# One tile and one rhythm for the modulation sums of a hybrid mLSTM and delta-rule block

## The chip, the cores and the metric

The kernel runs on one core of a Trainium2 chip. The metric is device time in microseconds of one execution. The core has TensorE (PE, with its weight loads as PEld), VectorE (DVE), ScalarE (ACT), GpSimd (POOL) and SyncE (SP); each works through its own instructions in the order in which the built program lists them, and they wait for each other through semaphores. In this kernel SP issues the loads of weights, POOL and ACT issue the smaller transfers to and from scratch memory in HBM.

## The reference, cut to what matters

One layer of a bidirectional encoder with 256 tokens and a width of 2048. Everything is float32.

```python
mod = c_act @ ada_w + ada_b                       # 6 x 2048 sums over 2048
shift_m, scale_m, gate_m, shift_f, scale_f, gate_f = jnp.split(mod[:, None, :], 6, axis=-1)
h = rms_norm(x, norm_mix_w) * (1 + scale_m) + shift_m
proj = h @ w_in                                   # 20 608 columns
...                                               # mLSTM (4 heads) -> y_a, gated delta rule (16 heads) -> y_b
x = x + gate_m * ((g_a * y_a + g_b * y_b) @ w_out)
hf = rms_norm(x, norm_ffn_w) * (1 + scale_f) + shift_f
gt, up = jnp.split(hf @ w_gate_up, 2, axis=-1)
x = x + gate_f * ((jax.nn.silu(gt) * up) @ w_down)
return rms_norm(x, norm_final_w)
```

The vector `mod` has six parts of 2048. Parts 0 and 1 are needed for the first projection. Part 2 (`gate_m`) is first used where the branch outputs are merged, parts 3 and 4 at the entrance of the feed-forward network (FFN), part 5 (`gate_f`) after it. The delta rule needs the inverse of a unit lower triangular matrix for each chunk and head.

## The kernel before, in words

**Products.** Each product in float32 is made of three products in a faster format: an operand is split into a high part (ACT copies it, `wh`) and a low part (DVE subtracts, `wl`). A weight tile of 1 MB (`raw`, three buffers) is split in two halves of 128 x 1024; each half takes one ACT copy, one DVE subtraction and 12 or 24 matmuls. A *job* (`fjob` for 128 columns, `tjob` for 512) is a generator that yields after every half; `fill(n)` advances the waiting jobs by n halves. `wh` and `wl` have three buffers each, so the splits can run up to three halves ahead of PE.

**Modulation sums.** Parts 2 to 5 are not made on PE. A row block of the transposed weights (128 x 2048, 1 MB) is loaded on SP's queue (`ask`, L116) and multiplied by the activated `c` and summed along the row in one DVE instruction (`add`, L124). There are 64 of them, 16 for each part. `pump` is called by every job after each half. With one tile, a sum is made when one is owed, the load is older than two halves and `held` is not set; the load for the next sum is asked for in the half after. `every` is the number of halves after which a sum is owed, 0 for none.

**Stages.** After the first projection (in which PE waits for loads) the delta rule goes in four groups g of four heads. Each group has: phase 1 of its heads (in the *pairs* of the group before), the inversion of its 32 x 32 blocks, and two pairs of heads (`gdn_phase2`). The inversion (`gdn_invert`, L704 and L710) is a chain of 60 small DVE instructions on the tile `uu`. Its last rows are stored by POOL to `inv_d` (L696), loaded again by POOL as the square tile `cg` (L723), transposed on DVE (L725) and mixed into the tile `R` (L729, L730, two instructions for each of two halves of `R`). The pair's first product on PE, `p1` (L761), reads the first half of `R` and the second, `p2` (L770), the other half. While the inversion and this round trip last, PE works on jobs: `invert` fills during the inversion, and `fill(8)` behind it.

Then comes the *border*: two mLSTM heads, the split of the delta rule's output (`obl`), the product with `w_branch_b` (`yb`), two more mLSTM heads, the product with `w_branch_a` (`ya`), the product with `w_out` (`o`), the FFN (`gt`, `up`, `d`).

**Sums by stage, before.** `every` is 1 in the pairs, 0 in inversions and `fill(8)`, 0 again at the start of the border, 1 from the third mLSTM head on, 4 in `ya` with a pool `sr` of three tiles that are asked for ahead, by explicit calls of `sums()` in the `o` jobs, and 8 in the FFN with one tile.

**Order.** A tile framework puts the instructions of each engine in an order by its own estimate of times; what is wrapped in `order(...)` keeps its place relative to the program. The order that was built, not the source, is what the engines follow.

Of the kernel before, what the change touches and what calls it, by code (L numbers as in the profile page):

```python
# [9 lines left out]
F32 = mybir.dt.float32  # L10
# [5 lines left out]
P = 128  # L16
T = 256
D = 2048
# [34 lines left out]
def hybrid_block(ctx: ExitStack, tc: tile.TileContext, xr, nfr, crow, pk_d, cst_d, ada2, ada4, win0, winb, wint, wba, wbb, wo, wgu, wd, out, dbg=None):  # L53
# [3 lines left out]
    def pool(stack, name, bufs=1, **kw):  # L57
        return stack.enter_context(tc.tile_pool(name=name, bufs=bufs, **kw))
# [3 lines left out]
    rows_p = pool(ctx, "rows")  # L62
# [9 lines left out]
    def order(ins, yes=True):  # L72

        return tc.keep_in_program_order(ins) if yes else ins
# [30 lines left out]
        order(S.activation(row_c[:, g * 512 : (g + 1) * 512], pc_, AF.Silu))  # L105


    room = [(rows_p, "ada", 1, 1)]
    asked, unasked, age = [], [], [0]

    def ask():

        pl, tag, bufs, _ = room[0]
        part, b = unasked.pop(0)
        raw = pl.tile([P, D], F32, tag=tag, bufs=bufs, name=f"ada{part}_{b}")
        order(nc.sync.dma_start(raw, ada4[part - 2, b]))  # L116
        asked.append((part, b, raw))
        age[0] = 0

    def add():  # L120

        part, b, raw = asked.pop(0)
        c = part * KB + b
        order(V.scalar_tensor_tensor(raw, raw, 1.0, row_c[:, :D], ALU.mult, ALU.mult, accum_out=mod[:, c : c + 1]))  # L124
        if b == KB - 1:
            c = slice(part * KB, part * KB + KB)
            V.tensor_tensor(mod[:, c], mod[:, c], pk[:, PK_ADAB + c.start : PK_ADAB + c.stop], ALU.add)
# [11 lines left out]
    def settle(keep=0, only=None):  # L139

        now = [f for f in behind if only is None or f.__name__ == only]
        for f in now[: len(now) - keep]:
            behind.remove(f)
            f()

    count, every = [0], [0]
    owed, held = [0], [False]

    def sums(n=1):

        while n and (unasked or asked):
            while unasked and len(asked) < room[0][3]:
                ask()
            add()
            n -= 1

    def pump():
        count[0] += 1
        age[0] += 1
        if every[0] and count[0] % every[0] == 0:  # L160
            owed[0] = 1
        if room[0][3] > 1:
            if owed[0]:
                owed[0] = 0
                sums()
        elif asked:
            if owed[0] and age[0] > 2 and not held[0]:
                owed[0] = 0
                add()
        elif unasked and every[0]:  # L170
            ask()

    def fjob(name, src, done):
# [95 lines left out]
    def fill(n=1):  # L269

        while n and fills:
            if next(fills[0], None):
                n -= 1
            else:
                fills.pop(0)
# [90 lines left out]
    def z_job(g, early=0):  # L366
        def done(ps):
            szs[g] = evp.tile([P, 2, 512], F32, tag="sz", bufs=1, name=f"sz{g}")
            for t in range(2):
                S.activation(szs[g][:, t], ps[t], AF.Silu)  # L370
        return tjob(f"z{g}", [wint[g, u] for u in range(4)], hh, hl, done, early)
# [121 lines left out]
    with ExitStack() as s0:  # L493
# [18 lines left out]
        def loads(b):  # L512
            ra = [w0.tile([P, D + 2], F32, tag="ra", bufs=5, name=f"ra{b}_{i}") for i in range(2)]
            raw = st.tile([P, N0, P], F32, tag="raw", bufs=3, name=f"raw0_{b}")
            for i in range(2):
                order(nc.sync.dma_start(ra[i], ada2[b, :, i]))
            order(nc.sync.dma_start(raw, win0[b]))
            return ra, raw
# [10 lines left out]
        ra, raw = loads(0)  # L529
# [18 lines left out]
        for b in range(KB):  # L548
            if b:
                ra, raw = loads(b)  # L550
# [137 lines left out]
    def gdn_invert(g):  # L688

        uu = uus.pop(g)  # L690
        tmp = bk.tile([64, 256], F32, tag="utmp", bufs=1, name=f"utmp{g}")
        inv = inv_d[g].rearrange("j b (x h) i -> h (b x) j i", h=GRP)

        def store(rows):
            for e in range(GRP):
                G.dma_start(inv[e, :, rows], uu[16 * e : 16 * e + 16, rows])  # L696

        yield
        order(V.memset(uu.rearrange("p j i -> p (j i)")[:, ::33], 1.0))
        size = 0  # L700
        for i in range(30, 0, -1):
            w = 31 - i
            t3 = tmp[:, 0 : i * w].rearrange("p (j c) -> p j c", j=i)
            order(V.tensor_tensor(  # L704
                t3,
                uu[:, 0:i, i : i + 1].broadcast_to([64, i, w]),
                uu[:, i : i + 1, i + 1 :].broadcast_to([64, i, w]),
                ALU.mult,
            ))
            order(V.tensor_tensor(uu[:, 0:i, i + 1 :], uu[:, 0:i, i + 1 :], t3, ALU.add))  # L710
            if i == 16:
                store(slice(16, 32))
            size += i * w + 125
            if size > 720:
                size = 0
                yield
        store(slice(0, 16))
# [300 lines left out]
    def invert(g):  # L1018
        gen = gdn_invert(g)
        next(gen)  # L1020
        fill(4 if g else 6)
        for _ in gen:
            fill(1)

    invert(0)
    for g in range(4):
        blocks = gdn_blocks(g)
        next(blocks)
        fill(8)
        next(blocks)  # L1030
        fill(1)
        pairs = [gdn_phase2(g, p) for p in range(2)]
        if g == 3:
            settle()
            sf.close()
            mq["pool"] = pool(sq_, "mq", side="right")
            first2 = [mlstm(h) for h in range(2)]
            for c in first2:
                next(c)
        every[0] = 1  # L1040
        for p in range(2):
            pieces = stream(4 * g + 2 * p + 4)
            for n in range(1, 10):

                held[0] = n < 4
                if p == 0:
                    next(blocks, None)
                next(pairs[p], None)
                if g == 3 and n == (8, 4)[p]:
                    next(first2[p])  # L1050
                for _ in range(last[n] if g == 3 else second[n] if p else after[n]):
                    next(pieces)
            for _ in pairs[p]:
                pass

            if g < 3:
                while 4 * g + 2 * p + 5 not in heads:
                    next(pieces)
        if g < 3:
            fills.insert(0, z_job(g + 1))  # L1060
            every[0] = owed[0] = 0
            invert(g + 1)
    settle()
    sx.close()
# [53 lines left out]
            yield from y_b(g)  # L1118

    o4s = [o_load(g) for g in range(2)]  # L1120
    every[0] = owed[0] = 0
    cores = steps(*first2)
    fill(1)
    next(cores)
# [19 lines left out]
    o_split(3, o4s[3])  # L1144
    fill(2)
    drive(cores, 3)
    every[0] = 1
    drive(steps(mlstm(2), mlstm(3)), 3)
    fill(1000)
    mgh, mgl = big(bigC, F32R, "mgh"), big(bigC, F32R, "mgl")  # L1150
    sm_.close()
    sr_ = ExitStack()
    if asked:
        add()
    room[0] = (pool(sr_, "sr"), "sr", 3, 3)
    gm = room[0][0].tile([P, D], F32, name="gm")
    dgs = {}

    def row_diag(part, g, rp):
        ms = mods[:, part == 5]  # L1160
        if not g:
            m = mod[:, part * KB : (part + 1) * KB]
            V.tensor_copy(ms[:, 0], m)
            V.tensor_tensor(ms[:, 1], m, ms[:, 0].bitcast(F32), ALU.subtract)
        dg = dgs[part, g] = rp.tile([P, 2, 4, P], F32R, tag="dg", bufs=2, name=f"dg{part}_{g}")
        for i in range(2):
            V.tensor_tensor(
                dg[:, i], ident.unsqueeze(1).broadcast_to([P, 4, P]),
                ms[:, i, 4 * g : 4 * g + 4].bitcast(F32).unsqueeze(2).broadcast_to([P, 4, P]), ALU.mult,
            )  # L1170
# [6 lines left out]
            PE.matmul(pr, onesr, woven(dg[:, i]), start=i == 0, stop=i == 1)  # L1177
        S.activation(woven(dst[:, g * 512 : (g + 1) * 512]), pr.rearrange("p (c h) -> p c h", h=2), AF.Copy)

    every[0] = 4  # L1180
    for g in range(4):
        for i, _ in enumerate(y_a(g)):
            if g and i == 3:
                merged(g - 1, mgh, mgl)
            if i in (1, 5) and g < 2:
                row_diag(2, 2 * g + i // 4, room[0][0])
            if i in (3, 7) and g < 2:
                row_spread(2, 2 * g + i // 4, gm)
    every[0] = 0


    def o_job(g, front=None):
# [112 lines left out]
    for g in range(4):  # L1305
        if g == 3:
            root()
        for i, _ in enumerate(o_job(g, front_o if g == 3 else None) if g else o_first, 0 if g else 2):
            if i in ((4, 7), (2, 5), (2, 5), (0, 2))[g]:
                sums()  # L1310
            if g == 3 and i == 4:
                sums(P)
                V.scalar_tensor_tensor(
                    affn, mod[:, 4 * KB : 5 * KB], 1.0, pk[:, PK_NFFN : PK_NFFN + KB], ALU.add, ALU.mult
                )
    if dbg is not None and "x1" in dbg:
        G.dma_start(dbg["x1"], x1)
    room[0] = (rows_p, "ada", 1, 1)
    ada_parts(5)
    sw.close()  # L1320
    sr_.close()
# [73 lines left out]
    for j in range(FB // 4):  # L1395
# [4 lines left out]
        for e2 in range(2):  # L1400
            px = gps(f"pxf{j}_{e2}")
            for e in range(2):
                f = 2 * e2 + e
                for t in range(2):
                    PE.transpose(px[:, e * T + t * P : e * T + (t + 1) * P], sg[:, t, f * P : (f + 1) * P], ident)
            b = 4 * j + 2 * e2
# [156 lines left out]
```

## Time and profile before

| | us |
|---|---|
| median of 3 runs | 1973.03 |
| lowest and highest run | 1969.95, 1974.28 |
| the profiled execution's own time | 1974.3 |
| its span | 1972.4 |
| PE busy | 1929.4 |
| DVE busy | 1405.5 |
| ACT busy | 1030.0 |
| the 64 modulation sums on DVE | 146.0 |
| mean granted clock of TensorE | 0.994 |

The profile's page says what each engine did in the span, which chain of work ended last, and which groups of instructions were the costliest. A busy PE is not a PE at its peak: matmuls overlap, and a matmul of 128 x 512 lasts 0.38 us while the next starts 0.22 us later. Where the start-to-start time grows, PE has lost time, and the view of waits tells for whom. The view of windows gives the busy time of each engine in a stretch and the granted clock there (1.00 is full speed).

### The profile page before, as it was taken

What the parts mean: (1) busy time and instruction counts of PE and PEld (TensorE: products, weight loads), DVE (VectorE), ACT (ScalarE), POOL (GpSimd) and SP (SyncE); (2) the same over time, 40 slices, a digit from 0 to 9 for tenths busy, and PEclk for the clock granted to TensorE, in tenths of its full rate; (3) what the DMA queues carried; (4) which work ended last, traced back from release to release, by engine and by line L of the source; (5) the groups of instructions that cost most, each with busy time, mean ns of one, the idle gap of its engine ahead of it and who ended that gap; (6) DMA issues with size and microseconds to landing.
All of it is one profiled execution on the core that took longest, in us unless ns stands there. A gap on an engine that the chain in (4) does not pass through costs nothing.

```text
span 1972.4 us, 27079 instructions
## 1 busy us (share of the span) xinstructions
PE 1929.4 (98%) x10418; PEld 1703.5 (86%) x10418; DVE 1405.5 (71%) x2067; ACT 1030.0 (52%) x1555; POOL 116.5 (6%) x211
## 2 busy tenths in 40 slices
PE   8999999999999999999999999999999999999998
PEld 6878889998998899889787888888888888888886
DVE  6779887887888798866577878866665665555554
ACT  3137656764766577565544444644444444444444
POOL 0001210111001010110100000200000000000000
PEclk9999999999999999999999999999999999999999
DMA  9987676766566666586777888566676665565663
GB/s 399 420 349 226 184 249 240 252 214 208 203 217 213 237 218 229 192 296 246 277 282 266 323 317 330 191 252 238 238 265 241 237 238 205 197 213 197 208 199 142
DMA packets 78962, 485.64 MB, mean 246 GB/s; under 512 B 10585, under 2 KB 15969, under 8 KB 24433
## 3 DMA queue, kind: packets, MB, share of 16 engines
q1 hardware_dynamic: 63216, 450.69, 62.9%
q0 software_dynamic: 8160, 17.88, 4.5%
q10 hardware_dynamic: 7458, 15.36, 2.1%
q8 instruction: 81, 1.33, 0.3%
q14 instruction: 47, 0.39, 0.1%
HBM read 467.07 MB, written 16.82 MB: 245 GB/s over the span
## 4 chain that ended last, share of the span: by engine, by line
PE 81%; DVE 8%; DMA 6%; ACT 2%; issue 1%; POOL 0%; ACTq 0%; SPq 0%; DVEq 0%; POOLq 0%
PE acc_gt L234 4%; PE acc_gt L235 4%; PE acc_gt L236 4%; PE acc_up L236 4%; PE acc_up L235 4%; PE acc_up L234 4%; PE acc_d L236 4%; PE acc_d L235 4%; PE acc_d L234 4%; DMA ra<-ada 3%; PE acc_b L187 2%; PE acc_b L188 2%; PE acc_b L189 2%; PE acc_o L236 2%; PE acc_o L234 2%; PE acc_o L235 2%
## 5 line engine op out<-in xcount | busy, mean ns | idle before, releaser
L215 DVE TENSOR_TENSOR wl_d<-raw_d,wh_d 128x1024 fp32r<-128x1024 f32 x88 | 107.7, 1224 | 105.9 <-ACT wh_d L213 105.9
L215 DVE TENSOR_TENSOR wl_up<-raw_up,wh_up 128x1024 fp32r<-128x1024 f32 x88 | 107.7, 1224 | 100.2 <-ACT wh_up L213 100.1
L215 DVE TENSOR_TENSOR wl_gt<-raw_gt,wh_gt 128x1024 fp32r<-128x1024 f32 x88 | 108.1, 1229 | 80.2 <-ACT wh_gt L213 80.2
L187 PE MATMUL acc_b<-hh,wh_b 128*128 128x256 f32 x576 | 163.0, 283 | 0.6 <-ACT wh_b L182 0.6
L189 PE MATMUL acc_b<-hh,wl_b 128*128 128x256 f32 x576 | 159.6, 277 | 0.8 <-DVE wl_b L184 0.8
L188 PE MATMUL acc_b<-hl,wh_b 128*128 128x256 f32 x576 | 159.2, 276 | 0.0
L213 ACT ACTIVATE wh_d<-raw_d 128x1024 fp32r<-128x1024 f32 x88 | 92.9, 1056 | 126.5 <-PE acc_d L235 117.7
L213 ACT ACTIVATE wh_gt<-raw_gt 128x1024 fp32r<-128x1024 f32 x88 | 92.9, 1056 | 118.6 <-PE acc_gt L235 71.1
L213 ACT ACTIVATE wh_up<-raw_up 128x1024 fp32r<-128x1024 f32 x88 | 92.8, 1055 | 108.1 <-PE acc_up L235 77.1
L124 DVE SCALAR_TENSOR_TENSOR ada<-ada,crow 128x2048 f32<-128x2048 f32 x64 | 146.0, 2284 | 0.0
L234 PE MATMUL acc_gt<-wh_gt,hfh 128*128 128x512 f32 x352 | 135.6, 385 | 0.6 <-ACT hfh L1350 0.6
L235 PE MATMUL acc_gt<-wh_gt,hfl 128*128 128x512 f32 x352 | 134.9, 383 | 0.0
L236 PE MATMUL acc_gt<-wl_gt,hfh 128*128 128x512 f32 x352 | 134.1, 381 | 0.0
L234 PE MATMUL acc_up<-wh_up,hfh 128*128 128x512 f32 x352 | 133.4, 379 | 0.0
L235 PE MATMUL acc_up<-wh_up,hfl 128*128 128x512 f32 x352 | 133.4, 379 | 0.0
L236 PE MATMUL acc_up<-wl_up,hfh 128*128 128x512 f32 x352 | 133.4, 379 | 0.0
L234 PE MATMUL acc_d<-wh_d,ffh 128*128 128x512 f32 x344 | 130.5, 379 | 0.0
L235 PE MATMUL acc_d<-wh_d,ffl 128*128 128x512 f32 x344 | 130.5, 379 | 0.0
L236 PE MATMUL acc_d<-wl_d,ffh 128*128 128x512 f32 x344 | 130.4, 379 | 0.0
L561 PE MATMUL first<-x,raw 128*128 128x256 f32 x512 | 114.5, 382 | 7.2 <-ACT x L555 7.2
L561 PEld LDWEIGHTS first<-x,raw 128*128 128x128 f32 x512 | 96.0, 190 | 25.7 <-ACT x L555 13.3
L189 PEld LDWEIGHTS acc_b<-hh,wl_b 128*128 128x128 f32 x576 | 111.3, 193 | 1.0 <-DVE wl_b L184 1.0
(383 smaller groups left out, 5263.1 us busy)
## 6 DMA issues: line engine op xcount, KB each, us to landing
ada<-ada SPq DMA_DIRECT2D x64, 1024.0 KB, 6.0
raw_gt<-wgu SPq DMA_DIRECT2D x44, 1024.0 KB, 4.9
raw_up<-wgu SPq DMA_DIRECT2D x44, 1024.0 KB, 4.9
raw_d<-wd SPq DMA_DIRECT2D x44, 1024.0 KB, 4.9
raw_b<-winb SPq DMA_DIRECT2D x36, 1024.0 KB, 5.3
ra<-ada SPq DMA_DIRECT2D x32, 1025.0 KB, 15.8
raw<-win SPq DMA_DIRECT2D x16, 1024.0 KB, 14.5
raw_z<-wint SPq DMA_DIRECT2D x16, 1024.0 KB, 5.0
```

Of the source, the lines that this page charges most:

```text
L124: order(V.scalar_tensor_tensor(raw, raw, 1.0, row_c[:, :D], ALU.mult, ALU.mult, accum_out=mod[:, c : c + 1]))
L187: PE.matmul(o, wh[:, k], woven(hh[:, kk]), start=kk == 0, stop=False)
L188: PE.matmul(o, wh[:, k], woven(hl[:, kk]), start=False, stop=False)
L189: PE.matmul(o, wl[:, k], woven(hh[:, kk]), start=False, stop=kk == KB - 1)
L213: order(S.activation(wh, raws[u][:, k0 : k0 + 2], AF.Copy), early)
L215: order(V.tensor_tensor(wl, raws[u][:, k0 : k0 + 2], wh.bitcast(F32), ALU.subtract), early)
L234: order(PE.matmul(ps[t], xh[:, kk, c], woven(wh[:, k]), start=kk == 0, stop=False), early and steps > 1)
L235: PE.matmul(ps[t], xl[:, kk, c], woven(wh[:, k]), start=False, stop=False)
L236: PE.matmul(ps[t], xh[:, kk, c], woven(wl[:, k]), start=False, stop=kk == last)
L561: PE.matmul(first[o], raw[:, o], x[:, b], start=b == 0 and o % 2 == 0, stop=b == KB - 1 and o % 2 == 1)
```

## The change

The pool of three tiles is gone, and so are `room` and the explicit `sums()` in the `o` jobs. One tile serves all sums, and `pump` alone makes them. The rhythm is kept on from the moment a group's inversion has been emitted (`every` 1, `held` off before `fill(8)`), through the border, `yb`, `ya` and the first `o` job. A new number `calm` says how many halves must pass between a sum and the load for the next one: 3 in the pairs of groups 0 to 2, otherwise 1; so a sum is due every six halves there and every four halves elsewhere.

```diff
-    room = [(rows_p, "ada", 1, 1)]
@@ ask
-        pl, tag, bufs, _ = room[0]
         part, b = unasked.pop(0)
-        raw = pl.tile([P, D], F32, tag=tag, bufs=bufs, name=f"ada{part}_{b}")
+        raw = rows_p.tile([P, D], F32, tag="ada", name=f"ada{part}_{b}")
@@
-    owed, held = [0], [False]
+    owed, held, calm = [0], [False], [1]
@@ sums
-            while unasked and len(asked) < room[0][3]:
+            if not asked:
                 ask()
@@ pump
-        if room[0][3] > 1:
-            if owed[0]:
-                owed[0] = 0
-                sums()
-        elif asked:
+        if asked:
             if owed[0] and age[0] > 2 and not held[0]:
-                owed[0] = 0
+                owed[0] = age[0] = 0
                 add()
-        elif unasked and every[0]:
+        elif unasked and every[0] and age[0] >= calm[0]:
             ask()
@@ for g in range(4):
         blocks = gdn_blocks(g)
         next(blocks)
+        every[0], held[0] = 1, False
         fill(8)
@@
-        every[0] = 1
+        calm[0] = 3 if g < 3 else 1
         for p in range(2):
@@
             every[0] = owed[0] = 0
+            calm[0] = 1
             invert(g + 1)
@@ the border
     o4s = [o_load(g) for g in range(2)]
-    every[0] = owed[0] = 0
+    held[0] = False
@@
     drive(cores, 3)
-    every[0] = 1
     drive(steps(mlstm(2), mlstm(3)), 3)
@@ before ya
-    if asked:
-        add()
-    room[0] = (pool(sr_, "sr"), "sr", 3, 3)
-    gm = room[0][0].tile([P, D], F32, name="gm")
+    sr = pool(sr_, "sr")
+    gm = sr.tile([P, D], F32, name="gm")
@@ ya
-    every[0] = 4
     for g in range(4):
...
-    every[0] = 0
@@ o jobs
-            if i in ((4, 7), (2, 5), (2, 5), (0, 2))[g]:
-                sums()
-            if g == 3 and i == 4:
+            if g == 3 and i == 3:
+                every[0] = owed[0] = 0
                 sums(P)
```

More of the change, by code (lines that the diff above doesn't have):

```diff
@@ L1185, in hybrid_block @@
             if i in (1, 5) and g < 2:
-                row_diag(2, 2 * g + i // 4, room[0][0])
+                row_diag(2, 2 * g + i // 4, sr)
             if i in (3, 7) and g < 2:
                 row_spread(2, 2 * g + i // 4, gm)
-    every[0] = 0
     def o_job(g, front=None):
@@ L1317, in hybrid_block @@
         G.dma_start(dbg["x1"], x1)
-    room[0] = (rows_p, "ada", 1, 1)
     ada_parts(5)
```

## The prediction

> **What bounds the kernel now.** I read the page first, then PE's waits from 290 to 1260 us (the delta rule to the entrance of the FFN, where every moved sum lies), then DVE and PE in order of time at the border and behind the inversions.
>
> ```profile
> span 1972.4 us, 27079 instructions
> PE 1929.4 (98%) x10418; PEld 1703.5 (86%) x10418; DVE 1405.5 (71%) x2067; ACT 1030.0 (52%) x1555; POOL 116.5 (6%) x211
> PE 81%; DVE 8%; DMA 6%; ACT 2%; issue 1%; POOL 0%; ACTq 0%; SPq 0%; DVEq 0%; POOLq 0%
> L124 DVE SCALAR_TENSOR_TENSOR ada<-ada,crow 128x2048 f32<-128x2048 f32 x64 | 146.0, 2284 | 0.0
> ada<-ada SPq DMA_DIRECT2D x64, 1024.0 KB, 6.0
> ```
>
> PE carries 81% of the chain that ended last. The change neither adds nor removes a matmul, a sum or a load: it can only change what PE waits for. In the stretch these are PE's waits that the change touches (total, times, longest):
>
> ```profile
> PE acc_ya L236 <- DVE wl_ya L215: 3.8, 2, 2.2
> PE acc_z L234 <- ACT wh_z L213: 2.5, 1, 2.5
> PE acc_ma L236 <- DVE wl_ma L215: 1.6, 2, 0.9
> PE acc_o L236 <- DVE wl_o L215: 1.1, 2, 0.8
> PE p L770 <- DVE pt L762: 1.0, 1, 1.0
> PE acc_b L189 <- DVE wl_b L184: 0.8, 1, 0.8
> PE acc_b L187 <- ACT wh_b L182: 0.6, 1, 0.6
> PE pb L819 <- DVE r L820: 0.6, 2, 0.3
> ```
>
> All of it is 12.0 us, and two of the waits cost more than they show, because the granted clock falls behind them:
>
> ```profile
> 1083.74 0.59 PE L1177 MATMUL row<-dg,onesr 128*128 128x512 f32 x2
> 1086.49 0.93 PE L236 MATMUL acc_ya<-wl_ya,hah 128*128 128x512 f32 x2 [2.15 <-DVE wl_ya L215]
> 793.28:796.69 3.41, 3.24 (x7) 2.15 (x8) 1.86 (x2) 3.33 (x9) 1.97 (x4) 0.50 0.11 19
> 1086.85:1090.20 3.35, 3.35 (x9) 2.60 (x8) 3.15 (x4) 1.14 (x2) 0.00 (x0) 0.50 0.98 306
> ```
>
> In the last two rows (windows) the third number from the right is the clock: 0.50 for 3.4 us after the waits of 2.5 and 2.15 us. In 3.4 us at half clock only half the work gets done, so each such window costs 1.7 us more. [...]
>
> **The change, part by part.** Positions are those of the changed program as built.
>
> *The ya border, removed.* Three sums stand back to back ahead of a split:
>
> ```profile
> 1080.80 2.29 DVE L124 SCALAR_TENSOR_TENSOR ada<-ada,crow 128x2048 f32<-128x2048 f32 x1
> 1083.01 2.28 DVE L124 SCALAR_TENSOR_TENSOR ada<-ada,crow 128x2048 f32<-128x2048 f32 x1
> 1085.22 1.22 DVE L215 TENSOR_TENSOR wl_ya<-raw_ya,wh_ya 128x1024 fp32r<-128x1024 f32 x1
> ```
>
> A sum costs DVE 2.21 us from start to start. In the changed order one sum stands between two splits, and the `dg` instructions that held up the second `wl_ya` stand behind later splits. Gain: the row of 3.8 and one half-clock window, -5.5. With one sum per four halves the splits keep their lead on PE; if they did not, the same 3.8 would return. The `o` jobs, with nine sums before, keep two; those that leave stood beside residual additions: -0.3, the smaller of the two waits in the `acc_o` row.
>
> *Pairs.* Groups 0 to 2 keep four of six sums; the one ahead of `r` (L820) goes: -0.6. Nothing else there is PE's wait on a sum.
>
> *Behind the inversions, added.* Group 0 gets two sums in DVE's idle time, and one split moves ahead of a mix of `R`: -0.7, the first of the `acc_ma` waits. In groups 1 and 2, though, the built order puts two sums *inside* the end of the inversion, and more splits too (group 1: two more, group 2: three more). DVE has no room there, and much behind it (DVE's busy time is the third one):
>
> ```profile
> 443.00:475.00 32.00, 30.24 (x139) 25.84 (x139) 30.59 (x66) 16.79 (x18) 2.25 (x4) 1.00 0.60 202
> 475.00:492.00 17.00, 17.00 (x117) 15.90 (x115) 8.03 (x10) 6.66 (x10) 4.21 (x8) 1.00 0.72 241
> ```
>
> Group 1, the end of the inversion, the square's arrival, the first half of `R`, the load's issue, `p1`:
>
> ```profile
> 469.62 1.21 DVE L215 TENSOR_TENSOR wl_o<-raw_o,wh_o 128x1024 fp32r<-128x1024 f32 x1
> 474.64 0.17 DVE L710 TENSOR_TENSOR uu<-uu,utmp 64x30 f32<-64x30 f32 x1
> 489.73 0.71 DVE L725 STREAM_TRANSPOSE cg<-cg 128x512 f32<-128x512 f32 x1 [3.62 <-DMA cg<-inv_d]
> 490.71 0.48 DVE L730 SCALAR_TENSOR_TENSOR R<-cg,cst,R 128x256 f32<-128x256 f32 x1
> 482.32 1.99 POOL L723 DMA_DIRECT2D cg<-inv_d  x4 [5.00 <-DMA inv_d<-uu]
> 471.23 0.38 PE L236 MATMUL acc_o<-wl_o,hh 128*128 128x512 f32 x1
> 491.79 0.98 PE L761 MATMUL p<-R,cc 128*128 128x32 f32 x8
> ```
>
> Before, `R` is ready at 491.2 and PE comes to `p1` at 491.8. After, the inversion ends 2 x 2.21 + 2 x 1.13 = 6.7 us later (1.13 is a split's pitch on a full DVE: two take 2.35 in a row below, one 1.22), and with the same 15.1 us to the square `R` is ready at 497.9. The split of 469.62 comes 1.7 us later (a sum less two small steps) where it led PE by 0.4: PE loses 1.2. The changed order puts ten matmuls of the next job (1.1 us) ahead of `p1`, so PE arrives at 491.8 + 1.2 + 1.1 = 494.1 and waits 3.8. With a half-clock window, 1.7, and without the old waits behind it (`p` L770, `acc_b` twice: 2.4) the group costs 1.2 + 3.8 + 1.7 - 2.4 = +4.3.
>
> Group 2, with group 0's load beside it:
>
> ```profile
> 656.99 0.17 DVE L710 TENSOR_TENSOR uu<-uu,utmp 64x30 f32<-64x30 f32 x1
> 670.55 0.71 DVE L725 STREAM_TRANSPOSE cg<-cg 128x512 f32<-128x512 f32 x1 [1.08 <-DMA cg<-inv_d]
> 674.94 0.97 PE L761 MATMUL p<-R,cc 128*128 128x32 f32 x8
> 665.26 1.99 POOL L723 DMA_DIRECT2D cg<-inv_d  x4 [5.52 <-DMA inv_d<-uu]
> 299.99 1.99 POOL L723 DMA_DIRECT2D cg<-inv_d  x4 [5.08 <-DMA inv_d<-uu]
> 309.56 0.71 DVE L725 STREAM_TRANSPOSE cg<-cg 128x512 f32<-128x512 f32 x1 [3.74 <-DMA cg<-inv_d]
> ```
>
> The inversion ends 2 x 2.21 + 3 x 1.13 = 7.8 later, the square comes at 678.4, and with one split put between the mixes the first half of `R` is ready 2.6 later, 681.0. PE arrives at 674.9 plus 22 matmuls (2.5), 677.4: a wait of 3.6, with the window +5.3.
>
> The square's load itself takes 5.4 us after its issues in group 1 (482.32 + 1.99 to 489.73), 3.3 in group 2 and 7.6 in group 0, where a sum's load (1 MB, 6.0 us) is under way. After, such loads are under way in groups 1 and 2 as well. The bounds are 0 (more traffic won't make it shorter) and 2.2 + 4.3; I take +1.5 in all, nearer to the groups' own rows.
>
> *Group 3* gets one sum inside (and two splits), and one between the mixes:
>
> ```profile
> 832.61 0.18 DVE L710 TENSOR_TENSOR uu<-uu,utmp 64x30 f32<-64x30 f32 x1
> 848.04 0.71 DVE L725 STREAM_TRANSPOSE cg<-cg 128x512 f32<-128x512 f32 x1 [0.18 <-DMA cg<-inv_d]
> 857.25 0.38 PE L236 MATMUL acc_mb<-wl_mb,hh 128*128 128x512 f32 x1
> ```
>
> The square comes at 848.0 + 4.5 = 852.5; transpose, mixes, split and sum ahead of the second `wl_mb` take 6.7, so it is ready at 859.2, and PE used it at 857.25: +2.0. Just before, one of four table loads of ACT goes and `wh_z` stands earlier, which can save up to the `acc_z` row and its window (-4.2); but the inversion that follows sets the pace, so only what starts that earlier counts, some 1.3. Together +0.7, between -4.2 and +2.0.
>
> *The border's first half.* Before, no sum stood between the pairs and the second `yb` job. Now three stand in `yb0` and one in `yb1`, beside the mLSTM heads' work, where
>
> ```profile
> 977.99 2.35 DVE L215 TENSOR_TENSOR wl_yb<-raw_yb,wh_yb 128x1024 fp32r<-128x1024 f32 x2
> 980.79 0.38 PE L236 MATMUL acc_yb<-wl_yb,obh 128*128 128x512 f32 x1
> ```
>
> the first split (ready 979.2) leads PE by 1.6: 2.2 less 1.6 is 0.6, and up to 0.9 for mLSTM results that DVE takes from PSUM later. I take +1.0, between 0 and 1.5. Below 0 it can't go, as nothing is taken away there.
>
> *SP's queue.* There are 64 loads for sums before and after. In `ya` and `o` each now waits for the one tile, so for the last sum, and the weight tiles queued behind it wait too. Those need a buffer that a split *behind* that sum frees, so the sum's load adds nothing to their wait: 0. The load (6.0 us to landing) has three halves, 3 x 2.6 = 7.8 us, until its sum. If that cover goes, DVE stands still before a sum and every split behind it is late; bounded by rival 3. The pairs of group 3 and the FFN keep their sums' places: 0. The three freed tiles serve nothing else: 0.
>
> *Sum.* -5.5 - 0.3 - 0.6 - 0.7 + 4.3 + 5.3 + 1.5 + 0.7 + 1.0 = +5.7, against the profiled execution's 1974.3 (span 1972.4 and 1.9 around it). That is 1.3 above the median of the runs, on which I put the forecast: 1973.0 + 5.7 = 1978.7. (0.2%, about what a measurement of this kernel can tell from no change, is 3.9 us.)
>
> **The rivals.**
> 1. *The cover holds* (faster). If the squares arrive 3.8 and 3.6 us earlier than summed, PE never waits for `R`. For it: DVE idles behind the inversions, and before, PE did not wait there. Against: the order is fixed, and DVE is at 30.6 of 32. Then groups 1 and 2 give 1.2 - 2.4 and 0, and `acc_z` its full -4.2: -5.5 - 0.3 - 0.6 - 0.7 - 1.2 - 4.2 + 1.0 = -11.5, 1961.5.
> 2. *The clock stays up* (no change). The two waits for `R` are there but cost no half-clock windows, and the loads none of their 1.5: +5.7 - 3.4 - 1.5 = +0.8, 1973.8. For it: of the two `acc_ya` waits the other, 3.8 - 2.2 = 1.6, stands in no half-clock window of the trace. Against: 2.15 did. [...]
> 3. *Loads collide* (slower still). All squares take group 0's 7.6 (+2.2, +4.3, and in group 3 up to 2.7): +5.7 - 1.5 + 9.2 = +13.4, 1986.4. For it: the DMA share is 0.60 to 0.72 there already. Against: groups 1 and 2 before had 1 MB loads beside them too.
>
> **How the numbers follow.** Forecast 0.55, rivals 0.15, 0.18, 0.12. The forecast's own spread is +2 to +9 (1975 to 1982); 0.05 of it lies within 0.2%. So faster 0.16 (rival 1 and a little), within 0.2% 0.23 (rival 2 and that), slower 0.61. The range leaves out rival 1 and the end of rival 3: 1969 to 1987.
>
> **What would show it.** Right: `p1` of groups 1 and 2 waits 3 to 6 us for `R`, with half clock behind it; the last `uu` to `cg` stays 13 to 17 us; no wait and no half clock at `ya`; sums of 2.2 us between the last steps of `uu`. Wrong: `p1` without a wait, or new waits in `yb` and `ya` for splits held up by a late sum's load.

## The result, and the profile after

| | before | changed |
|---|---|---|
| median | 1972.8 us (4 runs, 1969.95 to 1974.28) | 1992.6 us (4 runs, 1990.99 to 1995.1) |
| ratio, with its 95% interval | | 1.0105 (1.0088 to 1.0122) |
| span of the profiled execution | 1972.4 us | 1991.4 us |
| mean granted clock | 0.994 | 0.989 |

The change costs 1.05%, some 20 us, where the forecast had 5.7. The line numbers of the changed kernel are lower by 2 to 11: L724 is the second instruction of a mix of `R`, L755 is `p1`, L209 the split of a `tjob`, L122 the sum. The page first, in which DVE's work and the sums' are what they were:

```profile
span 1991.4 us, 27081 instructions
PE 1936.1 (97%) x10418; PEld 1709.7 (86%) x10418; DVE 1405.4 (71%) x2067; ACT 1028.7 (52%) x1554; POOL 116.8 (6%) x211
```

The rows of PE's waits from 290 to 1260 us that bear on the change (total, times, longest):

```profile
PE p L755 <- DVE R L724: 12.0, 2, 6.8
PE acc_mb L230 <- DVE wl_mb L209: 5.8, 3, 4.3
PE acc_a L183 <- DVE wl_a L178: 2.3, 2, 2.0
PE acc_o L230 <- DVE wl_o L209: 1.7, 2, 0.9
PE acc_z L230 <- DVE wl_z L209: 1.7, 1, 1.7
PE pxa L988 <- DVE hal L993: 1.2, 1, 1.2
PE acc_yb L230 <- DVE wl_yb L209: 0.9, 1, 0.9
```

The wait for `R` is new and is the largest of all; the row of `acc_ya` is gone. The last two rows are new too; before, the view shows no wait of PE between 950 and 1062 us. In order of time, group 1 (first five rows) and group 2 (the rest): a sum, the last step of `uu`, the issue of the square's loads on POOL, its transposition, `p1`.

```profile
475.26 2.28 DVE L122 SCALAR_TENSOR_TENSOR ada<-ada,crow 128x2048 f32<-128x2048 f32 x1
478.71 0.17 DVE L704 TENSOR_TENSOR uu<-uu,utmp 64x30 f32<-64x30 f32 x1
487.28 2.00 POOL L717 DMA_DIRECT2D cg<-inv_d  x4 [5.88 <-DMA inv_d<-uu]
495.82 0.71 DVE L719 STREAM_TRANSPOSE cg<-cg 128x512 f32<-128x512 f32 x1 [5.25 <-DMA cg<-inv_d]
497.34 1.92 PE L755 MATMUL p<-R,cc 128*128 128x32 f32 x8 [5.22 <-DVE R L724]
665.64 2.28 DVE L122 SCALAR_TENSOR_TENSOR ada<-ada,crow 128x2048 f32<-128x2048 f32 x1
669.09 0.17 DVE L704 TENSOR_TENSOR uu<-uu,utmp 64x30 f32<-64x30 f32 x1
677.71 2.00 POOL L717 DMA_DIRECT2D cg<-inv_d  x4 [5.87 <-DMA inv_d<-uu]
686.59 0.71 DVE L719 STREAM_TRANSPOSE cg<-cg 128x512 f32<-128x512 f32 x1 [7.04 <-DMA cg<-inv_d]
689.12 1.91 PE L755 MATMUL p<-R,cc 128*128 128x32 f32 x8 [6.80 <-DVE R L724]
```

From the last `uu` to the square it is 17.1 us in group 1 (15.1 before) and 17.5 in group 2 (13.6 before). Eight matmuls of `p1` take 1.9 us in place of 1.0: they run at half clock. Four windows of the trace, with PE's busy time as the first pair of numbers and the clock as the third number from the right:

```profile
475.00:492.00 17.00, 17.00 (x119) 15.93 (x118) 12.14 (x14) 8.67 (x10) 4.22 (x8) 1.00 0.99 362
490.80:494.21 3.41, 1.32 (x12) 1.13 (x11) 0.00 (x0) 1.06 (x1) 0.00 (x0) 1.00 1.02 311
494.21:507.86 13.65, 10.52 (x49) 10.52 (x50) 5.33 (x9) 6.59 (x17) 0.00 (x0) 0.50 0.23 80
685.36:699.01 13.65, 9.89 (x46) 9.89 (x47) 5.46 (x9) 6.05 (x15) 0.00 (x0) 0.50 0.30 113
```

While group 1's square is on its way the DMA engines are taken to 0.99 with 362 GB/s (0.72 and 241 before). Behind each of the two waits the clock is halved for 13.65 us, four times the 3.41 of the windows before (up to 1300 us). PE is busy there for 10.52 and 9.89 us, and half of that is lost, by estimate: 5.3 and 4.9 us.

Where the time goes, from the starts of the same matmuls in both traces (changed less before, running total):

| up to | starts, before and after | difference | added in the stage |
|---|---|---|---|
| end of `pb` of group 0 | 344.52, 342.51 | -2.0 | -2.0 |
| `vps` behind group 1 | 580.27, 586.77 | +6.5 | +8.5 |
| `acc_ma` ahead of group 2 | 640.50, 645.35 | +4.9 | -1.6 |
| `vps` behind group 2 | 759.48, 776.30 | +16.8 | +11.9 |
| `p2` of group 3 | 859.40, 883.99 | +24.6 | +7.8 |
| 13th matmul on `wl_yb` | 980.79, 1006.78 | +26.0 | +1.4 |
| `pxa` of the mLSTM heads beside `yb` | 996.07, 1023.62 | +27.5 | +1.5 |
| first matmul of `ya` | 1077.70, 1103.56 | +25.9 | -1.7 |
| in `ya`, behind both old waits | 1105.32, 1125.15 | +19.8 | -6.0 |
| entrance of the FFN | 1257.16, 1276.38 | +19.2 | -0.6 |

The -1.6 ahead of group 2 and the -1.7 ahead of `ya` are one half-clock window each (581.65 and 1025.38 in the trace before) that the changed execution doesn't have.

### The profile page after: what moved, and what is told of

It is laid out like the page before. It is cut to its first block, busy times and chain, and to the rows that moved or that the text cites. A ratio compares the mean times of both kernels' runs of the same rounds, so it can differ in the third digit from the quotient of the medians.

```text
span 1991.4 us, 27081 instructions
## 1 busy us (share of the span) xinstructions
PE 1936.1 (97%) x10418; PEld 1709.7 (86%) x10418; DVE 1405.4 (71%) x2067; ACT 1028.7 (52%) x1554; POOL 116.8 (6%) x211
## 5 line engine op out<-in xcount | busy, mean ns | idle before, releaser
L209 DVE TENSOR_TENSOR wl_d<-raw_d,wh_d 128x1024 fp32r<-128x1024 f32 x88 | 107.7, 1225 | 105.9 <-ACT wh_d L207 105.9
L209 DVE TENSOR_TENSOR wl_up<-raw_up,wh_up 128x1024 fp32r<-128x1024 f32 x88 | 107.7, 1224 | 100.2 <-ACT wh_up L207 100.1
L209 DVE TENSOR_TENSOR wl_gt<-raw_gt,wh_gt 128x1024 fp32r<-128x1024 f32 x88 | 108.1, 1228 | 80.3 <-ACT wh_gt L207 80.3
L122 DVE SCALAR_TENSOR_TENSOR ada<-ada,crow 128x2048 f32<-128x2048 f32 x64 | 146.1, 2283 | 1.8 <-DMA ada<-ada 1.8
L182 PEld LDWEIGHTS acc_b<-hl,wh_b 128*128 128x128 f32 x576 | 113.7, 197 | 0.1
```

Source lines behind the costliest of these rows:

```text
L182: PE.matmul(o, wh[:, k], woven(hl[:, kk]), start=False, stop=False)
L209: order(V.tensor_tensor(wl, raws[u][:, k0 : k0 + 2], wh.bitcast(F32), ALU.subtract), early)
```

## The experiments

Two theories for the loss. A: the sums, and the splits that move up with them, hold up the last steps of `uu` on DVE. B: the sums' loads slow down the square's way through HBM. D stands for a loss in the new rhythm itself. All ratios are against the kernel before, 0.001 is 2.0 us.

| run | ratio | 95% interval |
|---|---|---|
| changed kernel, and once more (`again`) | 1.0105, 1.0095 | 1.0088 to 1.0122, 1.0080 to 1.0110 |
| `late` | 0.9972 | 0.9960 to 0.9983 |
| `begin_only` | 1.0108 | 1.0088 to 1.0127 |
| `sums_only` | 1.0055 | 1.0040 to 1.0070 |
| `loads_only` | 0.9991 | 0.9982 to 1.0001 |
| `g0_only` | 0.9980 | 0.9969 to 0.9990 |
| `g0_g3` | 0.9997 | 0.9987 to 1.0006 |
| `not_g3` | 1.0072 | 1.0057 to 1.0087 |
| `mid_fill` | 0.9995 | 0.9982 to 1.0008 |
| `calm1` | 1.0093 | 1.0076 to 1.0110 |
| `warm` | 1.0094 | 1.0077 to 1.0111 |
| `warm_more` | 1.0092 | 1.0070 to 1.0113 |

### The two halves of the change

`late` is the changed kernel without the start behind the inversion (and keeps six sums in the pairs, so that as many sums reach the border as it has places for):

```diff
-        every[0], held[0] = 1, False
         fill(8)
...
-        calm[0] = 3 if g < 3 else 1
+        every[0], calm[0] = 1, 1
```

> The change without its start behind the inversions: the rhythm starts at the pairs, with six sums a group there as before; the border, yb, ya and o keep the new rhythm on the one tile. Theory A (the loss comes from what DVE has to do inside the ends of the inversions) and theory B (it comes from the sums' 1 MB loads behind the inversions) both expect the loss gone and the gain at ya kept: about -7, 1966 us (1963 to 1969), p1 of groups 1 and 2 without a wait over 1 us, half-clock windows of 3.4 us only. Theory D (the new rhythm in the border and the pairs costs the time) expects 1980 us or more.

`begin_only` is the kernel before with that one line:

```diff
+        every[0], held[0] = 1, False
         fill(8)
```

> The kernel before with one line of the change, the start of the sums behind each inversion; border, ya and o as before. Theories A and B expect what the changed kernel has lost by the border, about +24 to +27 on the kernel before: 1997 us (1993 to 2001), with waits of 5 to 7 us for R at p1 of groups 1 and 2 and two stretches of 13.7 us at half clock. Theory D expects 1973 to 1978 us.

Both came out in the main as A and B have it: `late` is 5.5 us *faster* than the kernel before, `begin_only` 21 slower, a little less than the 24 to 27 expected. D falls. Of the clock the runs show the mean alone: 0.987 to 0.990 in `begin_only` and 0.993 to 0.996 in `late`, where the kernel before has 0.994 (16 runs); how long their single stretches at half clock were isn't shown. The whole loss hangs on one line; the rest of the change is a small gain. That gain isn't seen between `begin_only` and the changed kernel, but the intervals are too wide to say that it is gone there. In `late` no row of waits names `R` any more. Its new waits stand in `yb` and the mLSTM heads beside it:

```profile
PE acc_yb L230 <- DVE wl_yb L209: 1.6, 2, 0.9
PE pxa L988 <- DVE hal L993: 1.1, 1, 1.1
PE ph L972 <- DVE hs L975: 0.6, 1, 0.6
```

### DVE's work or the loads

`sums_only` does two sums behind each inversion on data that is there, without a load; `loads_only` issues two loads and makes no sum. What they do there is thrown away; the true sums come later, at their places in `late`, so `sums_only` makes 72 sums and `loads_only` 72 loads. As in the changed kernel, the two sums of `sums_only` stand inside the end of the inversion in groups 1 and 2; a third one, which the changed kernel makes there while the square is on its way, is left out.

```diff
+        if dry[0]:                                  # sums_only
+            asked.append((0, 0, rows_p.tile([P, D], F32, tag="ada", name=f"dry{count[0]}")))
...
+        if not part:
+            order(V.scalar_tensor_tensor(raw, row_c[:, :D], 1.0, row_c[:, :D], ALU.mult, ALU.mult, accum_out=mod[:, 95:96]))
+            return
```

```diff
+        if dry[0]:                                  # loads_only
+            order(nc.sync.dma_start(raw, ada4[0, count[0] % KB]))
+            asked.append((0, 0, raw))
...
+        if not part:
+            return
```

> As late, but behind each inversion DVE does the sums of the changed kernel on data that is there already (the results are thrown away; no load is issued for them): two in each group. Theory A: inversions end 6 to 8 us later, p1 of groups 1 and 2 waits 3 to 4 us, the square's load takes 3 to 5.5 us as before; 10 to 16 us above late, 1976 to 1982 us. Theory B: waits at p1 below 1.5 us, at most 4 us above late.

> As late, but behind each inversion the sums' loads of 1 MB are issued, two in each group, and no sum is made from them (the data is dropped and loaded again later). Theory A: the inversions end as before, the square comes up to 2 us later in group 1 and up to 4 us in group 2, most of it in slack: 0 to 4 us above late, 1966 to 1970 us. Theory B: 10 us or more above late, with waits of over 3 us at p1.

`sums_only` is 0.0083 above `late`, 16 us, at the upper end of A; `loads_only` 0.0019, 3.8 us, at the upper end of A's range for it and below a half of B's. So over the whole kernel the sums on DVE, with the splits that move up beside them, are the main cause. The rows of `sums_only` and then of `loads_only` (the wait, then the last `uu`, the square and `p1` of group 1 and of group 2):

```profile
PE p L763 <- DVE R L732: 6.5, 2, 4.8
479.09 0.18 DVE L712 TENSOR_TENSOR uu<-uu,utmp 64x30 f32<-64x30 f32 x1
492.68 0.71 DVE L727 STREAM_TRANSPOSE cg<-cg 128x512 f32<-128x512 f32 x1 [1.73 <-DMA cg<-inv_d]
494.20 1.08 PE L763 MATMUL p<-R,cc 128*128 128x32 f32 x8 [1.69 <-DVE R L732]
661.67 0.18 DVE L712 TENSOR_TENSOR uu<-uu,utmp 64x30 f32<-64x30 f32 x1
677.18 0.71 DVE L727 STREAM_TRANSPOSE cg<-cg 128x512 f32<-128x512 f32 x1 [5.19 <-DMA cg<-inv_d]
679.71 1.91 PE L763 MATMUL p<-R,cc 128*128 128x32 f32 x8 [4.81 <-DVE R L732]
```

```profile
PE p L763 <- DVE R L732: 1.3, 1, 1.3
473.63 0.18 DVE L712 TENSOR_TENSOR uu<-uu,utmp 64x30 f32<-64x30 f32 x1
490.68 0.71 DVE L727 STREAM_TRANSPOSE cg<-cg 128x512 f32<-128x512 f32 x1 [5.58 <-DMA cg<-inv_d]
492.20 1.08 PE L763 MATMUL p<-R,cc 128*128 128x32 f32 x8 [1.25 <-DVE R L732]
657.11 0.18 DVE L712 TENSOR_TENSOR uu<-uu,utmp 64x30 f32<-64x30 f32 x1
672.99 0.71 DVE L727 STREAM_TRANSPOSE cg<-cg 128x512 f32<-128x512 f32 x1 [3.39 <-DMA cg<-inv_d]
675.07 0.97 PE L763 MATMUL p<-R,cc 128*128 128x32 f32 x8
```

In group 2 the square takes 15.5 us from the last `uu` with the sums alone, 15.9 with the loads alone and 17.5 with both. With the loads alone that delay disappears in the time that `R` had to spare: `p1` doesn't wait. With the sums as well nothing is spare: the 2.0 us from 15.5 to 17.5 are the 2.0 from the wait of 4.8 to that of 6.8. In group 1 it takes both parts. With the sums alone the chain ends 4.6 us later than in `late`, but the square takes 13.6 us, PE waits 1.7 and the clock stays up (the eight matmuls of `p1` take 1.08 us, against 1.91 in group 2); with the loads alone the square takes 17.1 and PE waits 1.3; the changed kernel has the late chain and 17.1 us, and waits 5.2 with half clock behind it. This fits that the two parts, 16 and 4, are less than what both cost together, 24 to 26, though the intervals alone would leave that difference open. A's expectation of waits of 3 to 4 us in both groups was met in neither: they were 1.7 and 4.8. Why the square of group 2 takes 15.5 us without any load added (13.5 in `late`) isn't known. How much of A's part is the two sums and how much the splits that move up was not taken apart.

### The place, and the single groups

`mid_fill` starts at the sixth of the eight halves behind an inversion; in its built order the sum stands behind the last step of `uu`. `g0_only` and `g0_g3` are `late` with the start in group 0, or 0 and 3; `not_g3` is the changed kernel without it in group 3.

```diff
-        fill(8)                                     # mid_fill, against late
+        fill(5)
+        every[0], held[0] = 1, False
+        fill(3)
```

```diff
+        if not g:                                   # g0_only; g in (0, 3) in g0_g3; g < 3 in not_g3
+            every[0], held[0] = 1, False
         fill(8)
```

> As late, but the sums begin at the sixth of the eight halves behind each inversion. In the built order one sum stands in each group behind the last step of uu (or behind R in group 0), and no split moves into the inversion; one or two loads more are under way while the square is fetched. Theory A: the ends of the inversions as before, no wait over 2 us at p1; 0 to 3 us above late, still 2 to 6 below the kernel before. Rival (beginning in the jobs behind the inversion costs whatever the place): 8 us or more above late.

> As late, but the sums begin behind the inversion in group 0 (two sums, both behind the last step of uu). The changed kernel was 2.0 us ahead by the end of the pairs of group 0. Theory A: 0 to 2 us below late, that is 5 to 8 below the kernel before, as no step of an inversion is held up. Rival (any sum behind an inversion costs): 3 us or more above late.

> As g0_only, with the start behind the inversion in group 3 too: one sum and one more split inside the inversion, one sum in the wait for the square and one behind R. What group 3 costs alone. The forecast's term for it was +0.7; the trace of the changed kernel shows waits of 4.5, 2.1 and 1.9 us there, but with all DMA queues and the inversion late from before. By the forecast: 0 to 3 us above g0_only. By the trace of the changed kernel: 5 to 9 us above it.

> The changed kernel with the start behind the inversion in groups 0 to 2 alone. By the drift in the trace of the changed kernel (16.9 us behind the kernel before at the end of group 2, 24.6 in the middle of group 3): 6 to 9 us below again. By what group 3 cost alone (g0_g3 less g0_only): 2 to 5 us below again.

`mid_fill` costs 0.0023, 4.5 us over `late`: more than A's 3, about what the loads alone cost, and a fifth of the start at the first half. It makes one sum a group there, in place of two or three, so the two are not the same load; but no sum stands in the chain, and the loss goes down to that of the loads. Its group 2:

```profile
657.71 0.17 DVE L704 TENSOR_TENSOR uu<-uu,utmp 64x30 f32<-64x30 f32 x1
675.46 0.71 DVE L719 STREAM_TRANSPOSE cg<-cg 128x512 f32<-128x512 f32 x1 [5.26 <-DMA cg<-inv_d]
676.98 1.08 PE L755 MATMUL p<-R,cc 128*128 128x32 f32 x8 [1.15 <-DVE R L724]
```

The square takes 17.75 us there, no less than the 17.5 of the changed kernel, and PE waits 1.15 and not 6.8, at full clock (the eight matmuls of `p1` take 1.08 us, 1.91 in the changed kernel): with the chain on time, a slow square is nearly covered. Group 0 alone costs nothing that can be told (0.0008 above `late`, intervals overlap; 0 to 2 us *below* was expected). Group 3 costs 0.0017 (3.4 us) on top of `g0_only` and 0.0023 (4.5 us) in the changed kernel (`not_g3` against `again`). The first lies between the two expectations (0 to 3 and 5 to 9), the second is what the runs let one expect (2 to 5) and not the 6 to 9 of the drift. Both intervals are wide (about 3 and 4 us to either side). The rows of group 3 in the changed kernel:

```profile
864.46 2.01 POOL L717 DMA_DIRECT2D cg<-inv_d  x4 [5.97 <-DMA inv_d<-uu]
873.47 0.71 DVE L719 STREAM_TRANSPOSE cg<-cg 128x512 f32<-128x512 f32 x1 [8.27 <-DMA bc<-mal_d]
874.34 1.22 DVE L209 TENSOR_TENSOR wl_mb<-raw_mb,wh_mb 128x1024 fp32r<-128x1024 f32 x1
875.61 0.48 PE L230 MATMUL acc_mb<-wl_mb,hh 128*128 128x512 f32 x1 [4.33 <-DVE wl_mb L209]
```

The split that PE needs stands behind the square's transposition in DVE's order. The square comes late, so DVE waits 8.3 us and PE, which wants `wl_mb` and not `R`, waits 4.3 for it. (The row puts DVE's wait down to `bc`, another load on POOL's queue, but what the instruction reads is `cg`; its last load was issued at 866.0 and the slowest of the four took 7.3 us.)

### The rhythm in the pairs

```diff
-        calm[0] = 3 if g < 3 else 1                 # calm1
```

> The changed kernel with six sums in the pairs of each group, as before, in place of four. In the built order of group 3 the sum that stood between the mixes of R then stands behind them. By the drift of the changed kernel against begin_only (0 at the end of group 2, 4 to 5.5 us in group 3): 3 to 6 us below again, 15 to 18 above the kernel before. Rival (the fewer sums in the pairs pay there): 2 us or more above again.

`calm1` and `again` are the same (1.0093 and 1.0095), so six or four sums in the pairs make no difference that shows, and the expected 3 to 6 us below `again` didn't come: they were read from a different loss in group 3 in two single executions.

### The clock

Matmuls that nothing reads, ahead of `p1` of groups 1 and 2:

```diff
+        if not p and g in (1, 2):                   # warm; (0, 32, 38) in warm_more
+            warm = gps(f"warm{g}")
+            for _ in range((0, 22, 28)[g]):
+                order(PE.matmul(warm, onesr, hh[:, 0:2].rearrange("p k t -> p (k t)"), start=True, stop=True))
         p1 = gps(f"p1_{g}_{p}")
```

> The changed kernel once more, beside the three that follow: 0.9 to 1.2% above the kernel before. If the long stretches at half clock are a matter of where the waits fall, they come in other lengths than 13.7 us in this execution.

> The changed kernel with matmuls that nothing reads, put on PE ahead of p1: 22 in group 1 (4.8 us) and 28 in group 2 (6.0 us), inside the waits of 5.4 and 7.0 us that it has there. Theory A with the clock (the waits leave PE without work and the granted clock stays at half for 13.7 us behind them, which cost 5.0 and 4.7 us besides the waits): both long stretches go, 8 to 10 us below the changed kernel, which is 10 to 13 us above the kernel before. Rival (half clock comes from something else than PE's lack of work, such as the busy DMA engines): both stretches stay and the time is that of the changed kernel within 2 us, some 20 above the kernel before.

> As warm, with 32 and 38 matmuls (6.9 and 8.2 us) ahead of p1 in groups 1 and 2, so that PE has something to do until R is there, and is late itself by about 1.2 us in each. If half clock comes from PE's lack of work, none is left behind p1 of these groups: the changed kernel less 5.0 and 4.7 us of half clock, plus 2.5 us of matmuls too many: 5 to 9 us below again. Rival: half clock stays, and the time is 0 to 4 us above again.

Windows behind `p1` of groups 1 and 2, first in `again`, then in `warm_more`:

```profile
496.15:502.98 6.83, 4.64 (x21) 4.65 (x22) 3.92 (x7) 3.31 (x8) 0.00 (x0) 0.50 0.13 49
683.88:697.53 13.65, 8.56 (x40) 8.57 (x41) 5.46 (x9) 5.52 (x13) 0.00 (x0) 0.50 0.37 125
```

```profile
494.00:508.00 14.00, 14.00 (x105) 13.04 (x104) 6.15 (x10) 8.53 (x20) 0.00 (x0) 1.00 0.39 139
684.00:700.00 16.00, 15.12 (x123) 14.26 (x122) 9.12 (x16) 10.86 (x22) 0.00 (x0) 1.00 0.28 96
```

With work for PE the clock stays up (1.00 in both windows, 0.50 in `again`), though the square comes as late as in `again` (at 496.75 and 685.07, against 496.82 and 686.44): half clock there does come from PE's lack of work. In `warm`, where PE runs out of work 2.5 and 3.1 us before `R` comes, 3.41 and 6.83 us at half clock are left; its time, 1.0094, is that of the changed kernel, where 8 to 10 us less were expected. Between the two traces, `warm_more` gains 5.5 us on `again` from 455 to 839 us. But the times hardly show it: 1.0092 against 1.0095, and 1.9 us between the medians, where 5 to 9 were expected. In the profiled execution half clock at other places takes part of it back, by estimate: the 20.48 us of the two windows of `again` are 0.005 of the mean clock (half of 20.48 in 1990), and it is 0.993 against 0.991 there. Whether that holds for the other executions isn't known; their mean clock (0.993 to 0.997, against 0.989 to 0.992 of `again`) would let one expect more.

Not all half clock stands behind a wait. Ahead of the stretch at 1025.38 of the kernel before the profile shows PE busy without a break:

```profile
1022.04 2.73 PE L962 MATMUL pden<-ones,mdec 128*128 128x1 f32 x24
1021.97:1025.38 3.41, 3.41 (x30) 3.30 (x29) 2.50 (x8) 1.40 (x3) 0.00 (x0) 1.00 0.87 324
1025.38:1028.79 3.41, 3.41 (x10) 2.65 (x9) 1.16 (x2) 0.00 (x0) 0.00 (x0) 0.50 0.88 269
```

In the 3.41 us ahead of it stand 24 matmuls of a single column (`pden`, in the mLSTM heads, two such groups in a trace), which the profile counts as busy. Up to 1300 us the beginnings of half clock lie a whole number of steps of 3.413 us apart, in the trace before (581.65, 793.28, 1025.38, 1086.82 and 1260.90: 62, 68, 18 and 51 steps) and in that of the changed kernel (19.76, 494.21, 685.36, 876.50 and 1279.28: 139, 56, 56 and 118 steps). The other three `pden` groups, one before and two in the changed kernel:

```profile
949.25 2.73 PE L962 MATMUL pden<-ones,mdec 128*128 128x1 f32 x24
973.93 2.73 PE L956 MATMUL pden<-ones,mdec 128*128 128x1 f32 x24
1049.60 2.73 PE L956 MATMUL pden<-ones,mdec 128*128 128x1 f32 x24
```

The group at 1022.04 fell whole into one step, and the clock halved at the end of that step. Each of these three has the end of a step inside it (at 950.29, 975.49 and 1050.58, worked out from the beginnings above), with 1.69, 1.56 and 1.75 us as the larger part, and the clock stayed at 1.00. How the steps fall on the kernel differs between executions of one kernel (494.21 in the changed kernel and 496.15 in `again` are no whole step apart), so such a stretch need not come in each of them, and with it 1.7 us, by estimate (half of 3.41).

The price of the clock in the whole time stays open. An estimate: the mean clock of the runs was 0.9940 before (25 runs, in the measurement with `warm`) and 0.9898 in the changed kernel (four), so at most 0.0042 of 1990 us, some 8 of the 20, are work not done at half clock.

## Why the prediction was wrong

The direction and the mechanism were right, the size was not: +5.7 was forecast, +20 measured, outside of the range of 1969 to 1987. By its own steps:

- *The ya border, -5.5.* Right, and a little small: both waits and the half-clock window are gone, the stage gains 6.0; `o` gains 0.6 where -0.3 was said.
- *The border's first half, +1.0.* Too small: the stage loses 3.0 up to 1023.6 us, twice the upper bound of 1.5, the most at one place in the wait of 1.2 for an mLSTM head's result (`pxa`). That the whole border shows only +1.3 is luck: 1.7 come back because the half-clock window behind `pden` fell away.
- *Pairs, -0.6, and group 0, -0.7.* Together with what else group 0 has, -2.0 in the trace; neither can be told in the times (`calm1`, `g0_only`).
- *The inversions' ends, +6.7 and +7.8.* Right: in group 1 the last `uu` is at 478.71 where PE was 2.2 us early by then, so +6.3; in group 2 at 669.09 with PE 4.6 late, +7.5. PE's arrival at `p1` was right too: 492.1 and 682.3, which less the drift of -2.2 and +4.6 are 494.3 and 677.7, where 494.1 and 677.4 were forecast. What came behind was mis-sized three times:
- *The square's load, +1.5 in all.* It is the term that failed first. The way from `uu` to the square grew by 2.0 and 3.9 us in groups 1 and 2: 5.9, near the upper bound of 6.5. Of it 1.1 and 3.6 lie behind the issues of the load, the rest in the store ahead of it, to which the forecast gave nothing. I took the value nearest to the groups' own rows, though a row of the same trace, group 0's 7.6, showed the case that the change was about to make everywhere: a sum's load under way. The median of the square's four transfers was 6.7 us to landing where it had been 3.5:

```profile
cg<-inv_d POOLq DMA_DIRECT2D x4, 64.0 KB, 3.5
```

```profile
cg<-inv_d POOLq DMA_DIRECT2D x4, 64.0 KB, 6.7
```

(first before, then after, from 476 to 497 us). `R` waits for all four, and the slowest took 6.8 us in place of 5.5 in group 1 and 7.4 in place of 4.7 in group 2. So the waits were 5.2 and 6.8 and not 3.8 and 3.6, and rival 3, to which I gave 0.12, was the better half of the answer.
- *One half-clock window of 1.7 for each wait.* All windows of the trace before were 3.41 us (up to 1300 us), behind waits of up to 2.5 or behind `pden`. Behind the longer ones it was 13.65 us twice in this execution: 5.3 and 4.9 in place of 1.7 each, 6.8 us more. `again`, the same kernel, had 6.83 in group 1 and 13.65 in group 2. Rival 2 (the clock stays up) was refuted in the traces: 0.50 behind both waits. In the changed kernel PE had work without a break from 497.34 on, and the full clock came back at 507.86, 10.5 us later.
- *Group 3 and acc_z, +0.7.* By the medians its start behind the inversion costs 3.4 to 4.5, more than the bound of +2.0 (which the intervals still reach). The bound took the second `wl_mb`, used at 857.25, and passed over the first, which PE uses at 853.76 and which stands behind the transposition too. And it put the square at 852.5: less the 17.4 us by which PE is late there, it came at 856.1, 3.6 later, of which 2.3 are the way from `uu`. The gain at `acc_z` was there (-2.3 between 759 and 793 us) and was given back 29 us later to waits for `wl_z` (1.7) and `wl_a` (2.0), as the inversion sets the pace.

With the measured terms in place of mine the sum is 5.7 + 4.4 (loads) + 6.8 (clock) + 7.1 (group 3 in the trace) - 0.7 (group 0 and the pairs) + 2.0 (`yb`) - 1.6 - 1.7 (the two windows that fell away) - 0.5 (`ya`) - 0.3 (`o`) = +21, against 19.2 in the traces. Rival 1, faster, needed squares earlier by what they were in fact later. What would have shown it right, a wait of 3 to 6 us at `p1` with half clock behind it and 13 to 17 us from `uu` to the square, is there, at its upper end and beyond (5.2 and 6.8; 17.1 and 17.5).

## What to carry to other kernels

A step that is allowed to start "behind" a serial chain can be ordered into it: look at the built order, and count every engine step that it puts into the chain, together with those that move up. Where a chain ends in a transfer whose time is only just covered, the extra loads beside it hide as long as anything is spare and count in full from there on (2.0 us of the square and 2.0 of the wait in group 2); take the row of the case that the change creates, not the mean of the old ones. `late`, the changed kernel without that one start, beats both: 0.9972 of the kernel before (0.9960 to 0.9983).

## What the runs showed of the hardware

- In the changed kernel the clock halved after a window of 3.41 us in which PE was busy for 1.32 us (490.80 to 494.21), so PE was not without work for the whole of it. Up to 1300 us the stretches at half clock were 3.41 us long in the kernel before (five of them); 13.65 (two) and 3.41 (three) in the changed kernel; 6.83 and 13.65 behind the waits for `R` in `again`, 3.41 and 6.83 in `warm`.
- In the traces of the kernel before and of the changed one the beginnings of these stretches lie whole steps of 3.413 us apart. Where all 2.73 us of 24 matmuls of one column (`pden`), which the profile counts as busy, fell into one step, the clock halved at its end (1025.38 in the kernel before); in the three groups with at most 1.75 us in one step it stayed at 1.00.
- The length didn't follow from the wait alone: in group 1 it was 13.65 us behind a wait of 5.2 (changed kernel) and 6.83 in `again`, whose two waits were 6.4 and 7.5, and in group 2 of both 13.65.
- With the DMA engines at 0.99 (475 to 492 us), four transfers of 64 KB took 6.7 us in the median and 6.8 for the slowest, where they took 3.5 and 5.5 at 0.72.
